# A trunk kernel whose dt columns move beside V's, in products of 320 columns

## The chip, the cores and the metric

The kernel runs on one core of a Trainium2 chip. The metric is device time in microseconds (us), measured over several runs of the same program; beside it stands one profiled execution, whose trace has every instruction with its start, length and engine. The engines are TensorE (PE in the rows; PEld are its weight loads), VectorE (DVE), ScalarE (ACT), GpSimd (POOL) and SyncE (SP, which here issues nearly all DMAs).

## The reference

One layer of a bidirectional hybrid encoder on 512 tokens of width 1024, in float32:

```python
h = rmsnorm(x, pre_mix_norm[l])
proj = h @ w_in[l]
z, xbc, dt_raw, q, k, v, gates = split_cols(proj, IN_SPLITS)
y_ssd = ssd_branch(z, xbc, dt_raw, ...)
y_attn = window_attention(q, k, v, attn_sink[l], rel_bias_table) @ w_attn_out[l]
mixed = (g_ssd * y_ssd + g_attn * y_attn) @ w_o[l]
x = x + rmsnorm(mixed, post_mix_norm[l])
h = rmsnorm(x, pre_mlp_norm[l])
f = jnp.square(jax.nn.relu(h @ w_mlp_in[l])) @ w_mlp_out[l]
x = x + rmsnorm(f, post_mlp_norm[l])
```

Of the columns of `w_in`, two groups matter here. V has 256 (4 heads of 64). `dt_raw` has 64 (32 scan heads in two directions); the scan uses `softplus(dt_raw + dt_bias)`, with `a = -exp(a_log)`. The attention adds a bias that depends on the distance of two tokens alone: a table of 32 x 16, of which the kernel makes a row of 512 distances for each of the 16 heads.

## The kernel before

**Numbers.** Every float32 operand of the large products is split in two parts of a shorter type (fp32r): `hi` is a cast, `lo` is what the cast lost. A product is then three: hi by hi, lo by hi, hi by lo (`mm3`, L393; for V and dt the three are written out). The input is normalised and transposed in four blocks of 128 tokens (`norm_x`, L596): ScalarE and VectorE square one half of the columns each (L603, L604), GpSimd adds and raises to the power -1/2 (L605, L606), VectorE scales by the row factor and by the gain (L609), PE transposes (L391, from `tr`), ScalarE casts the high part (L404) and VectorE subtracts for the low part (L405). The gain row is spread over the partitions by two float32 products of one row (`self.gb`, in `start`).

**Stages.** `start` (L547) loads x and V's weights, issues warm-up products of zeros (`WARM`, and three more), spreads the gain and normalises block 0. Then `build` makes a list of quanta, which `run_quanta` (L512) runs in order: V for each of the four blocks (`v_quantum`), dt (`dt_quantum`), K (2), Q (2), then eight scan groups with attention, gates and more Q between, the output projections and the MLP. Small stages are hung onto a quantum's number with `at(q, fn)`, or `later(d, fn)` counted from the current one: the bias rows (`bias_rows`, L677) at 1, the constant columns (`vectors`, L652) at 4, dt's sums and rows of cumulated decay four and five behind dt.

- `v_quantum(t)` normalises block t + 1, then makes 24 products of 256 columns: the stationary operand is 128 x 128 of the transposed block (high or low), the moving one is V's weights, which `load_v` loads in four pieces of 256 KB (two 128-row tiles each), casts on ScalarE (L575) and subtracts on GpSimd (L576). The 24 go hi by hi, lo by hi, hi by lo, eight each. The result is copied to `V` by ScalarE (L710).
- `dt_quantum` uses the common path for weights (`chunk_raw`, L454, and `chunk_split`, kind "both", L468 and L469): dt's 64 columns, high and low beside each other, make a moving operand of 128 columns against the block's high part, and of 64 columns against its low part, 16 products for each block. `dt_math` adds the halves and the bias (L742, L743) and computes the softplus on VectorE and ScalarE.
- K, Q and the rest take `cm`: eight tiles of weights as the stationary operand, all 512 tokens as the moving one, 24 products. Their raw weights lie in three buffers (`wr`, `RAW`), the split ones in three (`wh`, `wl`, `SPL`), filled ahead by `prefetch`.
- `bias_rows` multiplies the table by a one-hot matrix of distances in one float32 product (33 rows, 16 x 512 out), copies it out on VectorE (L688) and writes it to DRAM (L690), from where each head's bias is loaded (L841).

**Order.** The program order isn't what runs. A `Planner` simulates all instructions with a cost for each, and `chain` fixes its order on every engine. PE takes the first ready product in program order, but stays with one kind (float32 or fp32r) while others have been ready for less than 4 us; the other engines, SP's DMA queue among them, go by deadlines counted back from PE. PSUM has eight banks: three for `pp`, five for `ps`, each used in rotation.

Of the kernel before, what the change touches and what calls it, by code (L numbers as in the profile page):

```python
# [10 lines left out]
F32 = mybir.dt.float32  # L11
# [8 lines left out]
NT = 4  # L20
# [8 lines left out]
LO_DOWN = "p", "p", "p", "vp"  # L29
WARM = 10  # L30

SCAN = dict(load=3, weigh=(-2, -0.5), states=(0, 1), prep=(0, 1.5, 3, 4.5), outs=(2.5, 5.5), rms=9, finish=12,
# [23 lines left out]
class Slots:  # L56
# [5 lines left out]
    def get(self, name, shape=(128, 512), dtype=F32):  # L62
        s = self.free.popleft()
        self.n += 1
        t = self.pool.tile(list(shape), dtype, tag=f"s{s}", name=f"{name}_{self.n}", bufs=1)
        self.tags[t.tensor.name] = f"s{s}", 1
        self.slot[id(t)] = (s, t)
        return t

    def put(self, *tiles):  # L70
        for t in tiles:
            self.free.append(self.slot.pop(id(t))[0])


class Planner:
# [169 lines left out]

    LEAD, TAIL = 1000, 1300

# [7 lines left out]
    def plan(self, wait=0.3):  # L255
# [12 lines left out]
        for _ in self.ins:  # L268
# [17 lines left out]
            t = self.when[n] = max(t, ready[n])  # L286
            c, locks = self.cost[n]
            end = t + c
            if e == "SP":
# [39 lines left out]
class Trunk:  # L329
# [217 lines left out]
    def start(self):  # L547
# [23 lines left out]

        def load_v(k):
            w, hi, lo = (get("wv", (128, 2, 256), d) for d in (F32, F32R, F32R))
            nc.sync.dma_start(w, self.d_w_in[k * 128:(k + 2) * 128, C_V:C_V + 256].rearrange("(k p) n -> p k n", p=128))
            nc.scalar.copy(hi, w)  # L575
            nc.gpsimd.tensor_tensor(lo, w, hi.bitcast(F32), op=ALU.subtract)  # L576
            put(w)
            self.wv.append((hi, lo))

        load_x(0)  # L580
        for k in range(0, 8, 2):
            load_v(k)
        for t in range(1, NT):
            load_x(t)
        self.gb = [self.bank("pp") for _ in range(2)]
        for j in range(2):
            self.mm(self.gb[j], one[:1], g[j][:1], True, True)
        for _ in range(3):
            self.mm(dummy[:, :128], self.zero, self.zero, True, True)
        put(one, *g)  # L590
        self.hb, self.h = self.wide()
        self.norm_x(0)
        self.prefetch(0)
        self.at(1, self.later_constants)
# [100 lines left out]

    def v_quantum(self, t):

        nc = self.nc

        def run(_):  # L700
            if t < 3:
                self.norm_x(t + 1)
            tok = slice(t * 128, (t + 1) * 128)
            ps = self.bank("ps")
            for a, b in ((0, 0), (1, 0), (0, 1)):
                for k in range(8):
                    self.mm(ps[:, :256], self.h[k][a][:, tok], self.wv[k // 2][b][:, k % 2], a + b + k == 0, b == 1 and k == 7)
            if t % 2 == 0:
                self.V.append(self.slots.get("V", (128, 2, 256)))
            nc.scalar.copy(self.V[t // 2][:, t % 2], ps[:, :256])  # L710
            if t == 3:
                for a in self.wv:
                    self.slots.put(*a)

        return Quantum([], run)

    def dt_quantum(self):

        def run(parts):
            ps = self.bank("ps")  # L720
            for t in range(NT):
                tok = slice(t * 128, (t + 1) * 128)
                for k in range(8):
                    hi, lo = self.h[k]
                    self.mm(ps[:, t * 128:(t + 1) * 128], hi[:, tok], parts[0][:, k], k == 0, False, True)
                    self.mm(ps[:, t * 128:t * 128 + 64], lo[:, tok], parts[0][:, k, :64], False, k == 7, True)
            self.dt_math(ps.rearrange("p (t n) -> p t n", t=4))

        return Quantum([(self.d_w_in[:, C_DT:C_DT + 64].rearrange("(k p) n -> p k n", p=128), 8, 64, "both")], run)

    def dt_math(self, ps):
        nc = self.nc
        get, put = self.slots.get, self.slots.put
        bias = self.const("dtb", [128, 2, 64])
        self.bcast_row(bias[:, 0], self.d_dt_bias, 64)
        self.bcast_row(bias[:, 1], self.d_a_log, 64)
        self.tables = [get("tables", (128, 2, 4, 64)) for _ in range(3)]
        self.ncs = self.tables[2][:, 0]
        self.dt, self.cs, self.dec, self.coef = (self.tables[i // 2][:, i % 2] for i in range(4))
        w = [get("dtw", (128, 4, 64)) for _ in range(6)]  # L740
        v, e, r, s2, p, al = w
        nc.vector.tensor_tensor(v, ps[:, :, :64], bias[:, 0].unsqueeze(1).to_broadcast([128, 4, 64]), op=ALU.add)  # L742
        nc.vector.tensor_tensor(v, ps[:, :, 64:], v, op=ALU.add)  # L743

        nc.scalar.activation(e, v, AF.Abs)
# [45 lines left out]

        self.later(4, sums)
        self.later(5, rows)

# [784 lines left out]
    def build(self):  # L1579
# [7 lines left out]
        self.gd = self.dp.tile([1024, 512], F32, name="gd")  # L1587
        self.at(1, self.bias_rows)
        self.at(4, self.vectors)
        self.at(6, self.scan_constants)  # L1590
        kv = self.kv_quanta()
        self.add(*[self.v_quantum(t) for t in range(NT)], self.dt_quantum(), *kv)
        self.add(self.q_quantum(0), self.q_quantum(1))
# [72 lines left out]
```

## Time and profile before

| | us |
|---|---|
| median of 3 runs | 1101.32 |
| lowest, highest | 1098.49, 1101.61 |
| profiled execution | 1102.03 |
| its span, first instruction to last | 1100.0 |
| PE busy in it | 1088.0 |
| ScalarE, VectorE, GpSimd busy | 636.6, 746.4, 774.0 |

The mean granted clock of TensorE over the span was 0.992 of full speed. The busy times overlap, so they don't add up. A row of the timeline gives start, length, engine, line, operation, output tile and input tiles, shape and count; several instructions of one kind in a row are merged. What stands in square brackets at its end is the time for which the engine idled before it, and what ended that.

### The profile page before, as it was taken

The numbers are of one execution on the slowest core, as the hardware profiler recorded it, in microseconds if no ns is written. First come the engines' busy times: TensorE is split into PE (matmuls) and PEld (weight loads), VectorE is DVE, ScalarE is ACT, GpSimd is POOL, SyncE is SP. The second block draws the span as 40 slices with busy tenths as digits, with TensorE's granted clock in tenths as the row PEclk, the third lists the DMA queues.
The fourth block names the chain that finished last, engine by engine and source line by source line (L and its number), as shares of the span: only waits on it lengthen the run. The fifth ranks groups of instructions, "written<-read, shape, count | busy, mean of one in ns | idle before, by whom it ended". The sixth has DMA issues, their size and how long they took to land.

```text
span 1100.0 us, 16840 instructions
## 1 busy us (share of the span) xinstructions
PE 1088.0 (99%) x5664; PEld 914.4 (83%) x5664; DVE 746.4 (68%) x1285; ACT 636.6 (58%) x1364; POOL 774.0 (70%) x965
## 2 busy tenths in 40 slices
PE   9999999999999999999999999999999999999997
PEld 7888888888888888888888878888888888888885
DVE  5467787798797696977788653335653665665787
ACT  5357777777766777676677632323555444444543
POOL 6245657666567898899899775512668978978844
PEclk9899999999999999999999999999999999999999
DMA  7344624535535555556574563535312621621532
GB/s 223 85 114 119 151 75 123 133 85 156 143 97 151 154 161 146 162 149 159 135 196 134 166 208 96 153 100 170 115 40 57 178 77 53 192 75 44 163 101 78
DMA packets 214646, 140.66 MB, mean 128 GB/s; under 512 B 11773, under 2 KB 193509, under 8 KB 214560
## 3 DMA queue, kind: packets, MB, share of 16 engines
q1 hardware_dynamic: 214412, 139.53, 45.5%
q8 instruction: 44, 0.72, 0.3%
q14 instruction: 42, 0.34, 0.1%
q10 hardware_dynamic: 148, 0.07, 0.0%
HBM read 130.85 MB, written 8.72 MB: 127 GB/s over the span
## 4 chain that ended last, share of the span: by engine, by line
PE 96%; DMA 2%; DVE 1%; issue 0%; POOL 0%; POOLq 0%; DVEq 0%; SPq 0%
PE pp L387 67%; PE ps L387 26%; PE ps L391 4%; DMA wd<-in_w_mlp_out 1%; DMA rstd<-rrow 0%; DVE yT L1189 0%; DVE x L1575 0%; DVE acc L1541 0%; DVE junk L609 0%; DVE ag L1568 0%; DVE wd L1459 0%; DVE yl L1236 0%; POOL wl L478 0%; POOLq L1662 0%; DVE wd L1460 0%
## 5 line engine op out<-in xcount | busy, mean ns | idle before, releaser
L387 PE MATMUL pp<-b,wh 128*128 128x512 f32 (+1 forms) x1840 | 565.1, 388 | 0.8 <-DVE h L1331 0.8
L478 POOL TENSOR_TENSOR wl<-wr,wh 128x256 fp32r<-128x256 f32 (+1 forms) x500 | 410.1, 849 | 165.8 <-ACT wh L474 152.0
L387 PEld LDWEIGHTS pp<-b,wh 128*128 128x128 f32 x1840 | 341.3, 188 | 68.8 <-issue 1.0
L387 PE MATMUL pp<-b,wl 128*128 128x512 f32 (+1 forms) x920 | 357.7, 389 | 0.0
L387 PEld LDWEIGHTS pp<-b,wl 128*128 128x128 f32 x920 | 173.4, 189 | 34.9 <-issue 0.3
L474 ACT CAST wh<-wr 128x1024 fp32r<-128x1024 f32 x131 | 136.7, 1044 | 99.2 <-PE pp L387 78.5
L1495 POOL TENSOR_TENSOR wl<-wd,wh 128x256 fp32r<-128x256 f32 x140 | 113.7, 843 | 36.9 <-ACT wh L1491 34.1
L387 PE MATMUL ps<-wh,fh 128*128 128x512 f32 (+1 forms) x196 | 75.5, 385 | 0.5 <-DVE acc L1541 0.5
L1491 ACT CAST wh<-wd 128x512 fp32r<-128x512 f32 x80 | 47.4, 622 | 48.5 <-PE pp L387 26.2
L387 PE MATMUL ps<-wl,fh 128*128 128x512 f32 (+1 forms) x196 | 75.4, 385 | 0.0
L387 PE MATMUL ps<-wh,fl 128*128 128x512 f32 (+1 forms) x196 | 75.4, 385 | 0.0
L1374 DVE SCALAR_TENSOR_TENSOR pp<-pp,r 128x512 f32<-128x512 f32 (+1 forms) x31 | 17.6, 567 | 63.1 <-ACT r L1371 63.1
L1114 ACT ACTIVATE n<-cb,tables 128x128 f32<-128x128 f32 x128 | 49.5, 394 | 16.6 <-DVE cb L1105 14.1
L1495 POOL TENSOR_TENSOR wl<-wt,wh 128x256 fp32r<-128x256 f32 x56 | 45.3, 841 | 9.9 <-PE ps L387 4.9
L1150 POOL TENSOR_TENSOR w<-w,E 128x256 f32<-128x256 f32 x48 | 41.2, 872 | 12.9 <-DVE w L1146 6.5
L946 DVE SCALAR_TENSOR_TENSOR u<-pp,cv,u 128x510 f32<-128x510 f32 (+1 forms) x64 | 47.7, 746 | 3.3 <-ACT u L942 2.1
L1115 ACT ACTIVATE m<-cb,tables 128x128 f32<-128x128 f32 x128 | 49.3, 392 | 0.0
L1044 POOL TENSOR_TENSOR xd<-x,tables 128x256 f32<-128x256 f32 x48 | 35.4, 756 | 16.9 <-ACT x L969 14.1
L866 ACT ACTIVATE P<-P,mx 128x384 f32<-128x384 f32 (+1 forms) x64 | 35.3, 555 | 17.3 <-DVE mx L863 12.2
L1110 ACT ACTIVATE rf<-rf,tables 128x128 f32<-128x128 f32 x128 | 42.5, 396 | 2.4 <-DMA rf<-csT 2.3
L387 PEld LDWEIGHTS ps<-wh,fh 128*128 128x128 f32 x196 | 36.8, 188 | 8.0 <-DVE acc L1541 0.7
L387 PEld LDWEIGHTS ps<-wh,fl 128*128 128x128 f32 x196 | 36.8, 188 | 7.4
(242 smaller groups left out, 2064.0 us busy)
## 6 DMA issues: line engine op xcount, KB each, us to landing
wr<-in_w_in SPq DMA_DIRECT2D x74, 512.0 KB, 4.5
wr<-in_w_mlp_in SPq DMA_DIRECT2D x32, 512.0 KB, 4.2
wd<-in_w_mlp_out SPq DMA_DIRECT2D x64, 256.0 KB, 3.5
rb<-csT SPq DMA_DIRECT2D x32, 256.0 KB, 4.0
rf<-csT SPq DMA_DIRECT2D x32, 256.0 KB, 5.4
wr<-in_w_ssd_out SPq DMA_DIRECT2D x14, 512.0 KB, 4.4
E<-csE SPq DMA_DIRECT2D x96, 64.0 KB, 4.3
x<-in_x SPq DMA_DIRECT2D x16, 256.0 KB, 5.3
```

Source lines behind the costliest of these rows:

```text
L387: self.nc.tensor.matmul(out, lhsT, rhs, start=start, stop=stop, skip_group_check=more)
L391: self.nc.tensor.transpose(out, src, self.ident[:n, :n])
L474: self.nc.scalar.copy(hi[:, :m], raw)
L478: engines[e].tensor_tensor(lo[:, c], raw[:, c], hi[:, c].bitcast(F32), op=ALU.subtract)
L946: nc.vector.scalar_tensor_tensor(u[:, a:e], ps[:, a + d:e + d], self.wtap(t, b), u[:, a:e], op0=ALU.mult, op1=ALU.add)
L1044: nc.gpsimd.tensor_tensor(v4(xd[:, d * 256:(d + 1) * 256]), v4(xs(c)), by_dir(self.coef, c)[:, d].unsqueeze(2).to_broadcast([128, 4, 64]), ...
L1110: nc.scalar.activation(v4(rf)[:, h], v4(rf)[:, h], AF.Identity, bias=ncs[:, 0, h:h + 1])
L1114: nc.scalar.activation(v4(n)[:, h], cb[:, 0], AF.Copy, scale=dt[:, 0, h:h + 1])
L1115: nc.scalar.activation(v4(m)[:, h], cb[:, 1], AF.Copy, scale=dt[:, 1, h:h + 1])
L1150: nc.gpsimd.tensor_tensor(wc, wc, E[:, d], op=ALU.add)
L1491: nc.scalar.copy(hi, w)
L1495: (nc.vector if e == "v" else nc.gpsimd).tensor_tensor(low[:, q], w[:, q], hi[:, q].bitcast(F32), op=ALU.subtract)
```

## The change

- `load_v` now takes up to three 128-row tiles of weights at a time (tiles 0 to 2, 3 to 5, 6 and 7) into one of the raw buffers `wr`, V's 256 columns and dt's 64 beside each other, with a DMA for each group of columns. Each tile of 320 columns is cast on ScalarE by itself; its low part is made on GpSimd or VectorE in turn (`LO_V`).
- `v_quantum` takes a list of blocks. The first quantum has blocks 0 and 1: hi by hi and lo by hi for the one and then for the other, and the products by the weights' low parts last for both. Blocks 2 and 3 follow in a quantum each. Every product has 320 columns; 24 for each block, as before. V's copy takes the first 256 columns, and VectorE adds dt's bias to the other 64.
- `dt_quantum` and its 64 products are gone; `dt_math` follows block 3, and its first addition of halves is gone.
- `start` loads x of block 1 ahead of V's weights in program order, normalises blocks 0 and 1, loads dt's constants, and has four warm-up products behind the gain in place of three. The norm of block 2 is issued inside block 0's products, that of block 3 inside block 2's.
- In the planner, an instruction of PE that starts before 5.3 us costs double.
- `bias_rows` moves from quantum 1 to quantum 3, which is now the first of K's. As there are two quanta fewer ahead of K, dt's sums and rows are hung five and six behind in place of four and five.

```diff
+LO_V = "pvpvpvpv"
...
-    LEAD, TAIL = 1000, 1300
+    COLD, LEAD, TAIL = 5300, 1000, 1300
...
             c, locks = self.cost[n]
+            c *= 2 if e == "PE" and t < self.COLD else 1
...
-        def load_v(k):
-            w, hi, lo = (get("wv", (128, 2, 256), d) for d in (F32, F32R, F32R))
-            nc.sync.dma_start(w, self.d_w_in[k * 128:(k + 2) * 128, C_V:C_V + 256].rearrange("(k p) n -> p k n", p=128))
-            nc.scalar.copy(hi, w)
-            nc.gpsimd.tensor_tensor(lo, w, hi.bitcast(F32), op=ALU.subtract)
-            put(w)
-            self.wv.append((hi, lo))
+        def load_v(k0, k1):
+            w = self.wp.tile([128, 1024], F32, tag="wr", name=self.name("wr"), bufs=RAW)
+            self.tags[w.tensor.name] = "wr", RAW
+            w = w[:, :(k1 - k0) * 320].rearrange("p (k n) -> p k n", n=320)
+            for a, b, c in ((0, 256, C_V), (256, 320, C_DT)):
+                nc.sync.dma_start(w[:, :, a:b], self.d_w_in[k0 * 128:k1 * 128, c:c + b - a].rearrange("(k p) n -> p k n", p=128))
+            for k in range(k0, k1):
+                hi, lo = (get("wv", (128, 320), F32R) for _ in range(2))
+                nc.scalar.copy(hi, w[:, k - k0])
+                (nc.vector if LO_V[k] == "v" else nc.gpsimd).tensor_tensor(lo, w[:, k - k0], hi.bitcast(F32), op=ALU.subtract)
+                self.wv.append((hi, lo))
 
         load_x(0)
-        for k in range(0, 8, 2):
-            load_v(k)
-        for t in range(1, NT):
+        load_x(1)
+        for k in range(0, 8, 3):
+            load_v(k, min(k + 3, 8))
+        for t in range(2, NT):
             load_x(t)
...
-        for _ in range(3):
+        for _ in range(4):
             self.mm(dummy[:, :128], self.zero, self.zero, True, True)
...
         self.norm_x(0)
+        self.dt_bias = self.const("dtb", [128, 2, 64])
+        self.bcast_row(self.dt_bias[:, 0], self.d_dt_bias, 64)
+        self.bcast_row(self.dt_bias[:, 1], self.d_a_log, 64)
+        self.dtv = get("dtw", (128, 4, 64))
+        self.norm_x(1)
...
-    def v_quantum(self, t):
+    def v_quantum(self, some, after):
...
-            if t < 3:
-                self.norm_x(t + 1)
-            tok = slice(t * 128, (t + 1) * 128)
-            ps = self.bank("ps")
-            for a, b in ((0, 0), (1, 0), (0, 1)):
-                for k in range(8):
-                    self.mm(ps[:, :256], self.h[k][a][:, tok], self.wv[k // 2][b][:, k % 2], a + b + k == 0, b == 1 and k == 7)
-            if t % 2 == 0:
-                self.V.append(self.slots.get("V", (128, 2, 256)))
-            nc.scalar.copy(self.V[t // 2][:, t % 2], ps[:, :256])
+            ps = [self.bank("ps" if t else "pp") for t in some]
+            for lowest in (False, True):
+                for t, p in zip(some, ps):
+                    tok = slice(t * 128, (t + 1) * 128)
+                    for a, b in ((0, 1),) if lowest else ((0, 0), (1, 0)):
+                        if (t, a, b) == (some[0], 1, 0):
+                            for u in after:
+                                self.norm_x(u)
+                        for k in range(8):
+                            self.mm(p[:, :320], self.h[k][a][:, tok], self.wv[k][b], a + b + k == 0, b == 1 and k == 7)
+            for t, p in zip(some, ps):
+                if t % 2 == 0:
+                    self.V.append(self.slots.get("V", (128, 2, 256)))
+                nc.scalar.copy(self.V[t // 2][:, t % 2], p[:, :256])
+                nc.vector.tensor_tensor(self.dtv[:, t], p[:, 256:320], self.dt_bias[:, 0], op=ALU.add)
             if t == 3:
                 for a in self.wv:
                     self.slots.put(*a)
+                self.dt_math()
...
-        nc.vector.tensor_tensor(v, ps[:, :, :64], bias[:, 0].unsqueeze(1).to_broadcast([128, 4, 64]), op=ALU.add)
-        nc.vector.tensor_tensor(v, ps[:, :, 64:], v, op=ALU.add)
...
-        self.later(4, sums)
-        self.later(5, rows)
+        self.later(5, sums)
+        self.later(6, rows)
...
-        self.at(1, self.bias_rows)
+        self.at(3, self.bias_rows)
...
-        self.add(*[self.v_quantum(t) for t in range(NT)], self.dt_quantum(), *kv)
+        self.add(self.v_quantum((0, 1), (2,)), self.v_quantum((2,), (3,)), self.v_quantum((3,), ()), *kv)
```

More of the change, by code (lines that the diff above doesn't have):

```diff
@@ L713, in run, with dt_math @@
                     self.slots.put(*a)
+                self.dt_math()
         return Quantum([], run)
[L717 to L731, printed above, removed]
+    def dt_math(self):
         nc = self.nc
         get, put = self.slots.get, self.slots.put
-        bias = self.const("dtb", [128, 2, 64])
-        self.bcast_row(bias[:, 0], self.d_dt_bias, 64)
-        self.bcast_row(bias[:, 1], self.d_a_log, 64)
+        bias = self.dt_bias
         self.tables = [get("tables", (128, 2, 4, 64)) for _ in range(3)]
@@ L739, in dt_math @@
         self.dt, self.cs, self.dec, self.coef = (self.tables[i // 2][:, i % 2] for i in range(4))
-        w = [get("dtw", (128, 4, 64)) for _ in range(6)]
-        v, e, r, s2, p, al = w
-        nc.vector.tensor_tensor(v, ps[:, :, :64], bias[:, 0].unsqueeze(1).to_broadcast([128, 4, 64]), op=ALU.add)
-        nc.vector.tensor_tensor(v, ps[:, :, 64:], v, op=ALU.add)
+        v = self.dtv
+        e, r, s2, p, al = [get("dtw", (128, 4, 64)) for _ in range(5)]
+        w = v, e, r, s2, p, al
         nc.scalar.activation(e, v, AF.Abs)
```

## The prediction

> **What bounds the kernel now.** The page first: its span, the granted clock in 40 slices (tenths of full speed), and the shares of the chain that ended last.
>
> ```profile
> span 1100.0 us, 16840 instructions
> ...
> PEclk9899999999999999999999999999999999999999
> ...
> PE 96%; DMA 2%; DVE 1%; issue 0%; POOL 0%; POOLq 0%; DVEq 0%; SPq 0%
> ```
>
> 96% of the chain that ends last runs through TensorE (PE). So time taken off PE is time off the kernel, unless something late takes its place. One slice of the clock row stands below nine tenths, the second, from 27.5 to 55 us. The profiled execution took 1102.03 us, 2.03 more than its span and 0.7 more than the median of the three runs, 1101.32; the sum below is made against the profiled one. About 0.3% (3.3 us) is what a measurement of this kernel can tell from no change.
>
> Second, PE's timeline of the first 45 us (start, length, engine, line, operands, count, idle before).
>
> ```profile
> 1.03 5.61 PE L387 MATMUL ps<-zero 128*128 128x128 f32 x26 [1.03 <-DVE zero L560]
> 6.57 1.98 PE L387 MATMUL pp<-g,one 1*128 1x512 f32 x4
> 8.71 3.35 PE L391 MATMUL ps<-ident,junk 128*128 128x128 f32 x16 [0.16 <-DVE junk L609]
> 11.72 3.45 PE L387 MATMUL ps<-wv,b 128*128 128x256 f32 x22
> 15.10 1.03 PE L387 MATMUL ps<-hot,tab 33*16 33x512 f32 x2
> 16.06 0.50 PE L387 MATMUL ps<-wv,b 128*128 128x256 f32 x2
> 17.65 1.29 PE L391 MATMUL ps<-ident,junk 128*128 128x128 f32 x8 [1.08 <-DVE junk L609]
> 18.69 3.12 PE L387 MATMUL ps<-wv,b 128*128 128x256 f32 x24
> 21.65 1.21 PE L391 MATMUL ps<-ident,junk 128*128 128x128 f32 x8
> 22.61 5.99 PE L387 MATMUL ps<-wv,b 128*128 128x256 f32 x48
> 28.44 0.63 PE L387 MATMUL pp<-b,wh 128*128 128x512 f32 x2
> ...
> 29.72 10.43 PE L387 MATMUL ps<-wh,b 128*128 128x128 f32 x64
> 39.96 0.77 PE L387 MATMUL pp<-b,wl 128*128 128x512 f32 x1
> ```
>
> Read down: 13 warm-up products (10 and 3; each float32 product is two passes, hence x26), the gain row's broadcast from 6.57, the transposes of blocks 0 and 1 from 8.71, V's 96 products of 256 columns (`ps<-wv,b`) from 11.72, with the bias product (`ps<-hot,tab`) and the transposes of blocks 2 and 3 between them, the first K products at 28.44, and then dt's 64 products (`ps<-wh,b`) from 29.72 until K resumes at 39.96. That is 10.24 us for a thin set of columns.
>
> Third, stretches of one or two times 3.41 us with the granted clock (stretch, length, PE busy and products, clock, DMA share, GB/s).
>
> ```profile
> 6.18:9.59 3.41, 3.22 (x14) 1.00 1.08 372
> 9.59:13.01 3.42, 3.42 (x18) 0.50 1.12 306
> 30.07:33.49 3.42, 3.42 (x33) 1.00 0.51 146
> 33.49:40.31 6.82, 6.82 (x33) 0.50 0.01 2
> 40.31:43.73 3.42, 3.42 (x9) 0.50 0.00 0
> 43.73:47.14 3.41, 3.41 (x16) 1.00 0.45 111
> ```
>
> The clock is at half from 9.59 to 13.01 and again from 33.49 to 43.73. The second time it falls right behind a stretch that holds dt's products alone, stays down while dt's go on, and comes back behind a stretch of K's. In the first case the stretch before it holds the broadcast, products with a single row.
>
> **The change part by part.**
>
> *dt's own products go.* The block of 10.24 us stands on PE with nothing else to run there: the K product behind it starts at its end. Removed: 10.24 us. If K's were otherwise late, this would be worth less, so I look at K's weights below.
>
> *K at half clock.* From 39.96 to 43.73 K's products run for 3.77 us at clock 0.5. By the clock half of that is lost, 1.9 us; by the counts (9 products against 16 in the next stretch) 44%, 1.65. I take 1.8 us. It goes only if dt's products are what pulls the clock down; that is the third rival.
>
> [...]
>
> *V's products grow from 256 to 320 columns.* Their price is read from widths on both sides: 256 columns take (28.44 - 22.61)/48 = 121 ns; 384 columns, in the first attention head, and 512, in a late piece of the chain, are here:
>
> ```profile
> 62.72 0.34 PE L387 MATMUL ps<-KH,Q 128*128 128x384 f32 x1
> 62.90 0.34 PE L387 MATMUL ps<-KL,Q 128*128 128x384 f32 x1
> ...
> 808.90 5.44 PE ps L387 x24
> ```
>
> 384 take 0.18 us from start to start and 512 take 5.44/24 = 227 ns. The three lie on a line; 320 by the line from 256 to 512 is 148 ns, and the bounds are 121 and 180 ns, 0 and 5.7 us for the 96. 96 x 148 = 14.2 us in place of 11.6: **2.6 us more**, all on PE.
>
> *What goes from V's stage.* It now lasts 28.44 - 11.72 = 16.72 us: 11.6 of products, 1.04 + 0.96 of transposes (17.65 to 18.69, 21.65 to 22.61), 0.96 of bias product, 0.65 lost to the half clock up to 13.01, 1.08 idle at 17.65, the rest 0.4 in switching. Why it idles stands in the rows of GpSimd (POOL) and VectorE (DVE):
>
> ```profile
> 10.59 4.22 POOL L576 TENSOR_TENSOR wv<-wv,wv 128x512 fp32r<-128x512 f32 x3 [1.00 <-ACT wv L575]
> 14.77 0.20 POOL L605 TENSOR_TENSOR rst<-ssq 128x1 f32<-128x1 f32 x1
> 15.04 0.54 POOL L606 TENSOR_TENSOR rst<-rst,mhalf 128x1 f32<-128x1 f32 x1
> ```
>
> ```profile
> 16.17 0.68 DVE L688 COPY rows<-ps 16x512 f32<-16x512 f32 x1 [1.31 <-PE ps L387]
> 16.77 1.38 DVE L609 SCALAR_TENSOR_TENSOR junk<-x,rst,pp 128x512 f32<-128x512 f32 x2
> ```
>
> GpSimd makes V's low parts until 14.81; block 2's power waits behind them until 15.58. VectorE then has block 2's scaling (L609) behind the copy of the bias rows (L688), which waits for the bias product: 16.77 instead of some 15.7, and PE waits for it. The change takes all three causes away. Low parts are split between GpSimd and VectorE, four each, and come last, after 32 products (4.7 us); blocks 0 and 1 together give 48 products, 7.1 us, as cover for block 2's norm; the bias product and its copy leave the stage. So the 1.08 us idle and 0.96 us bias go from here. New on the engines: eight casts of 320 columns on ScalarE in place of four of 512, between 0.6 us more (by columns, from the 0.62 us of the row below) and 2.5 us (if each costs as much as a wide one); I take 0.9, nearer the columns. And four subtractions on VectorE, at most 0.7 us each by the wider L688 copy; its four additions of dt's bias take the place of two wider ones. None of these reaches PE while it has V products to run; where they do, it is the late front below.
>
> *The start of V's stage.* The changed planner counts a PE instruction double up to 5.3 us, so by its clock the ten first warm-up products last until the gain row has come, and the broadcast follows them; it can move up by about 1 us, and four warm-up products come behind it. Against that, the first V weights arrive as 480 KB, not 256.
>
> ```profile
> 7.42 0.62 ACT L575 CAST wv<-wv 128x512 fp32r<-128x512 f32 x1 [0.60 <-DMA wv<-in_w_in]
> ```
>
> ```profile
> 13.00:14.00 1.00, 1.00 0.70 116
> ```
>
> Now the first cast waits for its DMA until 7.42. 224 KB more at 372 GB/s, the rate before 9.59, is 0.6 us, so 8.0. The part with dt's columns has rows of 256 bytes; dt's load had them too, and while it was in flight the engines moved 116 GB/s at 0.70 share, 166 at a full one (the second row). In all 256 KB more come ahead of blocks 2 and 3: 0.7 us by the better rate, 1.6 by the worse; I take 1.2. Block 2's norm shifts by that, inside 7.1 us of cover, so PE doesn't see it. dt's two constant rows also load here, 32 KB each, too little to count. The first product: earliest 9.6 (11.72, less 1.0 for the broadcast and 1.1 for block 1's transposes, if these come behind it), latest 12.6 (ScalarE's extra 0.9 all ahead of it). I take 11.2.
>
> *Sum of the stage.* 11.2 + 14.2 + 2.0 transposes + 0.2 switching = 27.6, and 0.9 more if the clock is again at half up to 13.01: 28.5. More dense products now fall into the stretch before 9.59, so I weigh both and take **K's start at 27.9**, 0.5 us earlier than 28.44. Ends: 26.0 (first product at 9.6, full clock) and 30.2 (first at 12.6, half clock to 13.01, 0.8 us of waiting).
>
> [...]
>
> *The bias product behind K.* Its 0.96 us stood partly in a stall; now it interrupts full K work: **1.0 us added** (0 if it fills a wait, 1.3 with two switches). The rows and tables behind it:
>
> ```profile
> 20.67 2.83 POOL L478 TENSOR_TENSOR wl<-wr,wh 128x256 fp32r<-128x256 f32 x4
> ```
>
> ```profile
> 67.55 1.04 PE L387 MATMUL ps<-dtw,cst 128*128 128x128 f32 x6
> ```
>
> The bias rows are first needed by the scores, at 62.72; with some 51 as their new time, a product between 28 and 40 leaves 10 us or more. On SP the write of the rows (L690) now waits later; behind it stand weight loads, three split chunks ahead of PE, 16 us of cover. dt's sums run at 67.55, 27.6 us after dt's products; the changed offsets leave five K and Q products of 5.44 us between, 27 us, as now. K's first weights are split from 20.67 to 23.50, 4.4 us before 27.9, and without dt's chunk GpSimd is free earlier. V's raw weights now share K's three buffers, so K's loads wait for V's casts and subtractions; the 4.4 us cover that. K is not late.
>
> *Further on.* One place has a DMA on the chain:
>
> ```profile
> 750.11 5.96 PE pp L387 x27
> 756.07 5.36 DMA wd<-in_w_mlp_out
> ```
>
> The transfer starts when PE's work ends at 756.07, so it moves with PE, and nothing is given back there.
>
> **Sum:** -10.24 - 1.8 - 0.5 + 1.0 = -11.5 us. 1102.03 - 11.5 = 1090.5; from the median, 1089.8. I forecast 1090.0, between the two.
>
> **The rivals.**
>
> *A clean front.* No half clock before 13 us and the first product at about 10: K starts at 26.4, 1.5 us sooner, 1088.5. For it: the warm-up products behind the broadcast. Against it: ScalarE has to cast V's parts and block 0's transposes in one queue.
>
> *A late front.* V's weights and block 2 come late enough to starve PE: K starts at 30.2, 2.3 us later, 1092.3. For it: rows of 256 bytes at half the rate ahead of x; against it: 7 us of cover.
>
> *The clock falls anyway.* If the half clock from 33.49 to 43.73 is tied to time and not to dt's products, it lies over K's. Of dt's block 6.47 us ran at half clock; at full clock it is 10.24 - 3.2 = 7.0 us, and only that is saved: -7.0 - 0.5 + 1.0 = -6.5, 1094.8. [...] Against it: both falls follow a stretch of thin products, and every other slice of the clock row stands at nine tenths or more.
>
> *Given back.* If one of the DMA steps on the chain, as at 756.07, hangs on an earlier transfer and not on PE, PE comes 11.5 us sooner and waits as much longer: 1101. The PE row right before it speaks against it.
>
> *Slower.* dt's narrow products cost 7.0 us for 32 x 192 columns, 1.14 ns a column, against 0.47 for 256. If 320 columns, no multiple of 128 as V's, K's and the scores' widths are now, are paid at the narrow rate, a product takes 365 ns and the 96 take 35 us, 20.8 more than in the sum: 1110.8. It decides from 300 ns a product on ((11.5 + 3.3)/96 above 148). Against it: the line through 256, 384 and 512.
>
> **How the numbers follow.** Forecast 0.57, clean front 0.18, late front 0.14, clock 0.06, given back 0.03, slower 0.02. The forecast's own range is 1088.9 to 1091.5. The range holds the first three with the run-to-run spread of about 1.5 us at its ends: 1086.5 to 1094.0; 0.11 is left out. Faster by over 0.3%, below 1098.0: the first four, 0.95. Within: 0.03. Slower: 0.02.
>
> **What would show it.** Right: no `ps<-wh,b` block of 64 products; 96 products of 320 columns about 148 ns apart; the first K product near 28 us; the granted clock full from some 13 us on; no idle before block 2's transposes; the bias product among K's. Wrong: a half clock over K (third rival), spacing near 300 ns (last), idle in V's stage over 1 us (late front), or new idle of PE behind 60 us, above all before attention scores, the scan's tables, or at 745 to 760.

## The result, and the profile after

The changed kernel takes 1094.52 us (median of six runs, 1092.37 to 1095.74); the kernel before, on the same chip in the same set, 1102.01 (1098.49 to 1103.70). The ratio is 0.9935 with a 95% interval of 0.9917 to 0.9953: 7.5 us, or 0.65%, faster. Forecast were 1090.0, in a range up to 1094.0; the direction is right, and over a third of the gain is missing.

The page of the changed kernel, its span, clock row and shares of the chain that ended last:

```profile
span 1090.6 us, 16726 instructions
...
PEclk9999999999999999999999999999999999999999
...
PE 29%; DVE 1%; issue 0%; POOLq 0%; POOL 0%; DVEq 0%
```

No slice of the clock row is below nine tenths any more. The row counts the time ahead of the first recorded clock as full: the page of `after_again`, below, shows nines as well, though its products ran at half rate up to 13.5 us. (The chain was followed back over some 30% of the span only, so its shares say less than those of before.) The profiled execution took 1092.37 us, the fastest of the six. It alone can't tell why the median is 2 us higher. PE's timeline in it:

```profile
1.03 4.63 PE L389 MATMUL ps<-zero 128*128 128x128 f32 x20 [1.03 <-DVE zero L562]
5.60 2.28 PE L389 MATMUL pp<-g,one 1*128 1x512 f32 x4
7.80 1.16 PE L389 MATMUL ps<-zero 128*128 128x128 f32 x8
8.80 1.61 PE L393 MATMUL ps<-ident,junk 128*128 128x128 f32 x12
10.90 0.78 PE L389 MATMUL pp<-wv,b 128*128 128x320 f32 x2 [0.48 <-ACT wv L582]
11.51 0.60 PE L393 MATMUL ps<-ident,junk 128*128 128x128 f32 x4
...
13.55 0.54 PE L389 MATMUL pp<-wv,b 128*128 128x320 f32 x2
...
19.03 4.86 PE L389 MATMUL ps<-wv,b 128*128 128x320 f32 x32
23.73 1.04 PE L393 MATMUL ps<-ident,junk 128*128 128x128 f32 x8
25.02 4.03 PE L389 MATMUL ps<-wv,b 128*128 128x320 f32 x24 [0.26 <-ACT b L406]
28.89 0.63 PE L389 MATMUL pp<-b,wh 128*128 128x512 f32 x2
29.45 1.03 PE L389 MATMUL ps<-hot,tab 33*16 33x512 f32 x2
...
52.01 0.28 PE L389 MATMUL ps<-KH,Q 128*128 128x256 f32 x1
...
799.18 0.39 PE L389 MATMUL ps<-wh,fh 128*128 128x512 f32 x1
```

dt's block of 64 is gone and the bias product stands among K's. The 32 products from 19.03 to 23.73 are 147 ns apart. V's first product starts at 10.90, but only four run before 13.55, between groups of transposes; from there PE is dense. In the kernel before, the first score and the first product of the MLP's second half stood here:

```profile
62.49 0.28 PE L387 MATMUL ps<-KH,Q 128*128 128x256 f32 x1
...
808.74 0.39 PE L387 MATMUL ps<-wh,fh 128*128 128x512 f32 x1
```

These marks cut both profiles in four:

| us | before | after | difference |
|---|---|---|---|
| to K's first product | 28.44 | 28.89 | +0.45 |
| K to the first score | 34.05 | 23.12 | -10.93 |
| first score to the MLP's second half | 746.25 | 747.17 | +0.92 |
| from there to the span's end | 291.3 | 291.4 | +0.1 |

So one stretch brings the whole gain, and K starts later, not earlier. In all later profiles the last stretch is 291.4 and the third 746.2 to 747.4; the second is again 23.1 where the bias product stands in K and the clock is full. What differs most from run to run is K's start.

### The profile page after: what moved, and what is told of

Read it like the earlier page. It is cut to its first block, busy times and chain, and to the rows that moved or that the text cites. A ratio compares the mean times of both kernels' runs of the same rounds, so it can differ in the third digit from the quotient of the medians.

```text
span 1090.6 us, 16726 instructions
## 1 busy us (share of the span) xinstructions
PE 1078.6 (99%) x5602; PEld 904.0 (83%) x5602; DVE 743.1 (68%) x1291; ACT 635.8 (58%) x1367; POOL 773.6 (71%) x964
## 5 line engine op out<-in xcount | busy, mean ns | idle before, releaser
L389 PEld LDWEIGHTS ps<-wl,fh 128*128 128x128 f32 x196 | 36.8, 188 | 7.3
```

What stands on the lines that cost most here:

```text
L389: self.nc.tensor.matmul(out, lhsT, rhs, start=start, stop=stop, skip_group_check=more)
```

## The experiments

Each table row is one kernel, with its median, the ratio to the kernel before in the same set (95% interval), and from its profile: when the broadcast of the gain ends on PE, and when K's first product starts. Sets 1 and 4 ran on one chip, 2 and 3 on others; what is compared by its median comes from one set.

| kernel | set | median us | ratio | broadcast ends | K starts |
|---|---|---|---|---|---|
| `narrow_back` | 1 | 1105.39 | 1.0037 [1.0024, 1.0050] | 6.81 | 38.98 |
| `wide_back` | 1 | 1101.36 | 1.0001 [0.9985, 1.0017] | 7.57 | 38.72 |
| `wv_first` | 1 | 1094.00 | 0.9934 [0.9913, 0.9956] | 7.60 | 31.09 |
| `after_again` (changed kernel) | 1 | 1094.38 | 0.9935 [0.9916, 0.9954] | 9.38 | 32.55 |
| `block3_first` | 2 | 1093.58 | 0.9939 [0.9922, 0.9955] | 7.88 | 30.49 |
| `cold_off` | 2 | 1092.39 | 0.9932 [0.9915, 0.9948] | 7.62 | 28.75 |
| `bias_first` | 2 | 1095.08 | 0.9954 [0.9938, 0.9969] | 9.38 | 33.16 |
| `one_by_one` | 2 | 1093.56 | 0.9940 [0.9925, 0.9956] | 9.38 | 30.62 |
| `both_first` | 3 | 1091.51 | 0.9918 [0.9901, 0.9935] | 7.69 | 28.48 |
| `both_cold_off` | 3 | 1092.54 | 0.9925 [0.9907, 0.9942] | 8.16 | 29.55 |
| `both_one` | 3 | 1091.99 | 0.9921 [0.9904, 0.9938] | 7.67 | 28.60 |
| `merge_only` | 3 | 1092.44 | 0.9923 [0.9906, 0.9940] | 8.05 | 30.02 |
| `warm14` | 4 | 1092.46 | 0.9921 [0.9906, 0.9937] | 7.93 | 28.89 |
| `cold_off_ten` | 4 | 1091.75 | 0.9918 [0.9901, 0.9935] | 7.40 | 28.86 |
| `both_warm14` | 4 | 1091.40 | 0.9913 [0.9897, 0.9930] | 8.19 | 29.45 |
| `after_third` (changed kernel) | 4 | 1093.54 | 0.9932 [0.9915, 0.9948] | 9.38 | 31.42 |

### Do dt's narrow products pull the clock down?

Both kernels run 64 more products at the end of V's stage, whose result nobody reads: the one in dt's old shape, the other 256 columns wide.

The one in dt's shape (`narrow_back`), then the wide one (`wide_back`):

```diff
+                extra = self.bank("ps")
+                for u in range(NT):
+                    tok = slice(u * 128, (u + 1) * 128)
+                    for k in range(8):
+                        self.mm(extra[:, u * 128:(u + 1) * 128], self.h[k][0][:, tok], self.wv[k][0][:, :128], k == 0, False, True)
+                        self.mm(extra[:, u * 128:u * 128 + 64], self.h[k][1][:, tok], self.wv[k][0][:, :64], False, k == 7, True)
```

```diff
+                for u in range(NT):
+                    extra = self.bank("ps")
+                    tok = slice(u * 128, (u + 1) * 128)
+                    for k in range(8):
+                        for i in range(2):
+                            self.mm(extra[:, :256], self.h[k][i][:, tok], self.wv[k][0][:, :256], k + i == 0, k == 7 and i == 1)
```

> The changed kernel with 64 extra products between V's and K's, 128 and 64 columns wide in turn, as dt's were; their result is not used. If narrow products pull the clock down: the block lasts about 10 us (full clock for its first 3 to 7 us, half clock behind), K's first products run at half clock until a stretch of 3.41 us is dense again, and the time is 10 to 13 us above the changed kernel's, 1104.5 to 1107.5. If the fall of the clock is tied to a time after the start: the clock stays full, the block lasts 7.2 us, and the time is about 1101.7.

> The changed kernel with 64 extra products in the same place, all 256 columns wide; their result is not used. If width decides: clock full throughout, 64 x 121 ns = 7.7 us more, about 1102.3, more columns than the narrow block in less time. If any 64 products more in this place bring the clock down, or the fall is tied to time: half clock over the block or over K's, 1105 or more.

Windows of `narrow_back`, then of `wide_back` (columns as in the prediction: stretch, length, busy time and instructions of PE, PEld, DVE, ACT, POOL, then clock, DMA share, GB/s):

```profile
31.24:34.65 3.41, 3.41 (x33) 3.41 (x33) 3.12 (x6) 0.34 (x1) 0.00 (x0) 1.00 0.61 163
34.65:48.31 13.66, 13.66 (x42) 10.02 (x42) 5.55 (x13) 0.41 (x2) 0.00 (x0) 0.50 0.18 46
48.31:51.72 3.41, 3.41 (x16) 2.81 (x15) 0.68 (x1) 1.34 (x2) 0.00 (x0) 1.00 0.17 61
```

```profile
32.83:36.24 3.41, 3.41 (x31) 3.41 (x30) 3.24 (x6) 0.00 (x0) 0.00 (x0) 1.00 0.50 148
36.24:39.65 3.41, 3.41 (x27) 3.24 (x26) 3.17 (x8) 0.00 (x0) 0.00 (x0) 1.00 0.00 0
```

Behind a stretch of 3.41 us full of narrow products the clock is at half for 13.66 us; behind one full of wide products, just as busy on PE (3.41 of 3.41 us), it stays at 1.00. Against `after_again` the narrow block costs 11.0 us and the wide one, with more columns, 7.0. The third rival, a clock that falls anyway, is out: the narrow products do it. (The narrow block also writes to one bank and the wide one to four; no run separates that from the width. Nor do 128 columns bring the clock down as such: the warm-up products, in float32, are 128 wide, and the full clock is recorded behind them, from 6.23 us in the changed kernel's profile.)

### Why does K start late?

Two places stand out in the changed kernel. First, ScalarE (ACT) and VectorE (DVE) ahead of block 3's products:

```profile
23.16 1.05 ACT L476 CAST wh<-wr 128x1024 fp32r<-128x1024 f32 x1 [2.18 <-DMA wr<-in_w_in]
24.12 0.36 ACT L726 COPY V<-ps 128x256 f32<-128x256 f32 x1
24.38 1.08 ACT L406 CAST b<-ps 128x512 fp32r<-128x512 f32 x2
```

```profile
25.62 0.17 DVE L653 COPY dcol<-dsk 64x16 f32<-64x16 f32 x1 [0.88 <-DMA dsk<-in_d_skip]
25.71 1.27 DVE L407 TENSOR_TENSOR b<-ps,b 128x512 fp32r<-128x512 f32 x2
```

ScalarE idles 2.18 us for K's second raw weights, with block 3's casts (L406) behind that in its queue; VectorE idles 0.88 us for the constants of d_skip, with block 3's subtractions (L407) behind. Neither is needed yet. Second, V's weights: the first cast waits for its load until 10.39, since SP issues x of blocks 0 to 2 ahead of the six loads.

```profile
10.39 1.18 ACT L582 CAST wv<-wr 128x320 fp32r<-128x320 f32 x3 [0.36 <-DMA wr<-in_w_in]
```

```profile
0.72 2.77 SPq L572 DMA_DIRECT2D x<-in_x  x6
3.78 4.45 SPq L579 DMA_DIRECT2D wr<-in_w_in  x6
8.27 1.18 SPq L572 DMA_DIRECT2D x<-in_x  x2
```

K's raw weights come late, by these rows because V's now lie in the same three buffers: SP issues K's loads right behind VectorE's last reads of them (14.00 + 0.56, and 15.46 + 1.28). In the kernel before, the first two went out at 13.09 and 14.31.

```profile
14.00 0.56 DVE L583 TENSOR_TENSOR wv<-wr,wv 128x320 fp32r<-128x320 f32 x1
...
15.46 1.28 DVE L583 TENSOR_TENSOR wv<-wr,wv 128x320 fp32r<-128x320 f32 x3
```

```profile
14.88 0.40 SPq L456 DMA_DIRECT2D wr<-in_w_in  x1
...
16.83 1.41 SPq L456 DMA_DIRECT2D wr<-in_w_in  x2
```

`wv_first` puts the loads of V's weights ahead of x of block 2 in SP's order:

```diff
+        for n in loads("x_")[4:8]:
+            key[n] = max(key[n], max(key[m] for m in loads("wr_")[:6]) + 1)
```

`block3_first` puts K's second and third cast behind block 3's last cast in ScalarE's order:

```diff
+        for n in writes("wh_")[1:3]:
+            self.turn[n].add(writes("b_")[7])
+            self.next[writes("b_")[7]].append(n)
```

> The changed kernel with V's weights issued on SP ahead of block 2's x, in place of behind it. If the start of V's stage is held by the landing of its weights: the first cast comes about 1.4 us earlier (9.0 in place of 10.4), V's products run without gaps from 12.5 in place of 14, K starts near 27.5, and the time is 1 to 1.5 us below the changed kernel's. If ScalarE's queue holds it, K's start stays at 28.9 and the time is the same.

> The changed kernel again. If the spread between its runs (1092.4 to 1095.7) comes from where a half-clock stretch falls in the first 20 us: a profile that is slower than 1093.5 shows a half-clock stretch of 3.4 us between 9 and 20 us, which the first profile lacks, and its K starts 1 to 1.7 us later. If not: the clock is as in the first profile and the time is lost elsewhere.

> The changed kernel with ScalarE's two casts of block 3 put ahead of the second of K's weight casts, which waits for its load. If this order is what makes PE wait ahead of block 3's products (0.3 to 2.3 us in four profiles): the wait falls below 0.4 us and the time by about 1.2 us, to 1093.2. If the wait is block 3's own norm, it stays and the time is the same.

Both moved the wait instead of removing it. In `wv_first` the first cast comes at 9.15 in place of 10.39, and V's stage is dense from 12.72 and not 13.55, though the clock there is at half from 9.08 to 12.49; but then PE waits for block 2 (first row); in `block3_first` the cast's wait is gone, and VectorE's wait for d_skip is 2.21 us and comes to the surface as 1.42 on PE (second and third).

```profile
16.92 1.29 PE L397 MATMUL ps<-ident,junk 128*128 128x128 f32 x8 [1.31 <-DVE junk L625]
```

```profile
26.93 0.44 DVE L659 COPY dcol<-dsk 64x16 f32<-64x16 f32 x1 [2.21 <-DMA dsk<-in_d_skip]
```

```profile
28.02 2.19 PE L395 MATMUL ps<-wv,b 128*128 128x320 f32 x13 [1.42 <-DVE b L413]
```

`after_again`, the changed kernel once more, showed something else. Its front in PE's timeline:

```profile
1.03 4.64 PE L389 MATMUL ps<-zero 128*128 128x128 f32 x20 [1.03 <-DVE zero L562]
5.60 3.78 PE L389 MATMUL pp<-g,one 1*128 1x512 f32 x4
9.31 2.08 PE L389 MATMUL ps<-zero 128*128 128x128 f32 x8
11.18 2.61 PE L393 MATMUL ps<-ident,junk 128*128 128x128 f32 x12
13.55 0.55 PE L389 MATMUL pp<-wv,b 128*128 128x320 f32 x2
...
21.41 4.86 PE L389 MATMUL ps<-wv,b 128*128 128x320 f32 x32
...
28.02 1.44 PE L389 MATMUL ps<-wv,b 128*128 128x320 f32 x8 [0.88 <-ACT b L406]
30.08 2.63 PE L389 MATMUL ps<-wv,b 128*128 128x320 f32 x16 [0.63 <-DVE b L407]
32.55 0.63 PE L389 MATMUL pp<-b,wh 128*128 128x512 f32 x2
```

The same 10 warm-up products end at 5.60, but the broadcast takes 3.78 us (2.28 in the first profile) and the 8 passes behind it 2.08 (1.16): PE still runs at half rate, and the first full clock is recorded at 13.50, not 6.23. K starts 3.7 us later: V's run of 32 products is 2.4 late (21.41 against 19.03), and the waits ahead of block 3 are 0.88 and 0.63 against 0.26.

### What makes the clock late: the doubled cost, the interleaving, the bias product?

`cold_off` takes the planner's doubled cost away. With it the broadcast goes after 10 warm-up products and four follow; without it 13 go ahead and one follows.

```diff
-    COLD, LEAD, TAIL = 5300, 1000, 1300
+    COLD, LEAD, TAIL = 0, 1000, 1300
```

`bias_first` hangs the bias product back onto V's stage:

```diff
-        self.at(3, self.bias_rows)
+        self.at(1, self.bias_rows)
```

`one_by_one` runs blocks 0 and 1 one behind the other (and hangs the small stages one quantum later, as there is one more):

```diff
-        self.add(self.v_quantum((0, 1), (2,)), self.v_quantum((2,), (3,)), self.v_quantum((3,), ()), *kv)
+        self.add(self.v_quantum((0,), ()), self.v_quantum((1,), (2,)), self.v_quantum((2,), (3,)), self.v_quantum((3,), ()), *kv)
```

> The changed kernel with the planner's doubling of early PE instructions set to zero, so that 13 warm-up products come ahead of the gain's broadcast, as before the change, not 10. If the earlier broadcast helps: up to 1 us slower, 1095.4. If ten warm-up products are too few to bring the clock up in some runs (in one profile it was at half until 13.5 us, and K started 3.7 us later than in another): the clock is full before 8 us in the profile, and the time is the same or up to 1 us lower, 1093.4.

> The changed kernel with the bias product back in the second quantum, among V's products. If its 1 us is paid wherever it stands: the same time within 0.5 us, 1094.4. If it fills a wait of PE in V's stage: 0.5 to 1 us faster, 1093.6. If its copy holds up VectorE ahead of a norm, as before the change: K starts 1 us later and the time is 1 us longer, 1095.4.

> The changed kernel with blocks 0 and 1 in quanta of their own, so that each block's products by the weights' low parts follow its own others. If the interleaving is cover that PE needs: idle of 1 us or more in blocks 0 and 1, K starts 1 to 2 us later, 1095.5 to 1096.5. If the weights' high parts bound the stage's start anyway: the same within 0.5 us.

Without the doubled cost the six runs lie between 1091.98 and 1093.07, the lowest median of the set (the changed kernel itself isn't in it); the clock is full from 4.23 us. `bias_first` and `one_by_one` have the doubled cost, and both profiles show the late clock (13.77 and 13.37). In `bias_first` K to the first score is 22.03, 1.09 less: the bias product's price in K, to be paid in V instead. Its median is the highest of the set, 1.5 us above the other two with the doubled cost; how much of this the place of the bias product makes isn't settled. In `one_by_one` PE idles only 0.24 ahead of block 3: the interleaving isn't needed to cover the norm.

### Both queue waits, and the change cut down

`both_first` holds back K's casts and the d_skip copies behind block 3; `both_cold_off` and `both_one` do so without the doubled cost, the second with the blocks one by one. `merge_only` keeps of the change only dt's columns in V's products, with their loading, dt's constants and block 1's norm in `start`: blocks one by one, bias product in V's stage, no doubled cost, and three warm-up products behind the gain in program order (in its trace all 13 run ahead of it).

```diff
+        hold = [(n, writes("b_")[7]) for n in writes("wh_")[1:3]] + [(n, writes("b_", "DVE")[7]) for n in writes("dcol", "DVE")]
+        for n, m in hold:
+            self.turn[n].add(m)
+            self.next[m].append(n)
```

> The changed kernel with two orders turned round: ScalarE's casts of block 3 ahead of the second of K's weight casts, and VectorE's subtractions of block 3 ahead of the copy of d_skip's columns. With the first alone PE's wait moved to the second queue (1.4 us for VectorE in that profile). If these two waits are what stands ahead of block 3's products: PE waits 0.4 us or less there, and the time is 1 to 1.5 us below the changed kernel's, 1093.2. If another wait takes their place: more than 0.8 us idle ahead of block 3's products, and no gain.

> The same with the planner's early doubling at zero as well. If the two effects are separate and the doubling costs the clock in some runs: narrow spread as in that kernel alone (1092.0 to 1093.1) and 0.3 to 1 us below it, 1091.8. If the early doubling only shifted the same wait: 1092.4 again.

> The same as the last, with blocks 0 and 1 in quanta of their own. If interleaving gives no cover that PE needs: the same time as the last within 0.5 us. If it does: 1 us slower or more.

> dt's columns beside V's alone: no early doubling, three warm-up products behind the gain, no interleaving, the bias product in the second quantum. If the merge brings nearly all of the gain: 1092 to 1095, 7 us or more below the kernel before. If the other parts bring 2 us or more: 1096 or more.

ScalarE in `both_first` shows the order that was wanted, block 3's casts (L412) ahead of K's (L482), with no wait for a load:

```profile
24.22 1.07 ACT L412 CAST b<-ps 128x512 fp32r<-128x512 f32 x2
25.18 2.01 ACT L482 CAST wh<-wr 128x1024 fp32r<-128x1024 f32 x2
```

PE idles 0.24 there. `both_cold_off` shows no further gain over the doubled cost's removal: in its profile the clock is at half from 8.76 to 12.18, and K begins at 29.55. Its expectation named a second outcome, that the doubled cost had only shifted the same wait, and the traces bear it out: in `cold_off`, `cold_off_ten` and `merge_only`, without these edits, PE idles 0.24 ahead of block 3 as well. VectorE in `cold_off` subtracts for block 3 (L407) ahead of the copies (L653) by itself:

```profile
25.11 1.29 DVE L407 TENSOR_TENSOR b<-ps,b 128x512 fp32r<-128x512 f32 x2 [0.43 <-ACT b L406]
26.31 1.24 DVE L653 COPY dcol<-dsk 64x16 f32<-64x16 f32 x2
```

So taking the doubled cost away changes the warm-up and the queues at once, and what the queue waits alone are worth in the median, some 1 us by `warm14` and `both_warm14` below, isn't settled. `merge_only` has the whole gain of the change: 0.9923 [0.9906, 0.9940] against 0.9935, intervals that overlap. Its K starts at 30.02, with the bias product ahead, and its first score at 52.05, as in the changed kernel's own profile (52.01).

### Warm-up products by count

`warm14` keeps the doubled cost and has 14 ahead of the broadcast and four behind; `both_warm14` is `both_first` with the same edit:

```diff
-WARM = 10
+WARM = 14
```

`cold_off_ten` is `cold_off` with ten in all, and all ten go ahead of the broadcast:

```diff
-WARM = 10
+WARM = 6
```

> The changed kernel with 14 warm-up products ahead of the gain's broadcast in place of 10, early doubling as in the change. If the doubling costs because ten products don't always bring the clock up: the profile's clock is full before 8 us, the spread narrows to about 1 us, and the median falls by 1 to 2 us below the changed kernel's of this job. If the doubling costs by the order that it makes elsewhere: no lower than the changed kernel.

> No early doubling, but only ten warm-up products ahead of the broadcast and none behind (13 and one without doubling otherwise). If ten are too few: the spread widens to 2 us or more and the median rises by 1 us or more over the kernel without doubling, 1093.5 to 1095. If the count doesn't matter: about 1092.4 with a spread of 1 us.

> The changed kernel with block 3's casts and subtractions ahead of the two waits, and 14 warm-up products ahead of the broadcast. If the two effects add: 2.5 to 3 us below the changed kernel of this job, 1091 to 1091.8, narrow. If one covers the other: as warm14.

> The changed kernel again, beside the three others on the same chip: 1094.4 with a spread of 2 to 3 us.

`warm14` removes the long runs: 1091.64 to 1092.95, against 1091.83 to 1094.91 in `after_third`, whose profile again shows the late clock (13.28). `both_warm14` has the lowest ratio of the study and is 2.1 us under `after_third` in the same set, but its interval overlaps those of `warm14` and `cold_off_ten`. `cold_off_ten` missed its expectation: with ten products ahead but no doubling its runs stay within 1091.29 and 1092.88.

The profiles together say more than each. The recorded clock changes in steps of 3.41 us (in the kernel before at 6.18, 9.59, 13.01, 33.49 and 43.73, one, one, six and three steps apart). Cut time in such steps, so that one ends where the first full clock is recorded. For the eight profiles below (ten products ahead, broadcast from 5.60), the step in which the broadcast begins holds so much warm-up:

| | step | warm-up in it | full clock from |
|---|---|---|---|
| `wv_first` | 2.25 to 5.67 | 3.35 | 5.67 (to 9.08) |
| `both_first` | 2.45 to 5.86 | 3.15 | 5.86 |
| changed kernel, `block3_first` | 2.82 to 6.23 | 2.78 | 6.23 |
| `after_third` | 3.04 to 6.45 | 2.56 | 13.28 |
| `one_by_one` | 3.13 to 6.54 | 2.47 | 13.37 |
| `after_again` | 3.26 to 6.67 | 2.34 | 13.50 |
| `bias_first` | 3.53 to 6.94 | 2.07 | 13.77 |

The table parts cleanly between 2.56 and 2.78 us, and in every other profile of the study a step ends before the broadcast begins, with 2.8 us of warm-up or more in it. So one reading of the first full clock fits all profiles: the broadcast's products, of a single row, count too little, as steps with 0.85 us of them or more (3.41 less 2.56) are not followed by the full clock and those with 0.63 or less are. At half rate the four passes then last 3.78 us and fill most of the next step as well (to 9.38), and the clock comes two steps late. At half rate a warm-up product lasts 0.46 us (4.64 for ten): by this reading 13 or 14 of them hold a step with 2.8 us of warm-up wherever the steps lie, ten leave about three positions in ten without one (worked out from these rows, an estimate). Where the steps lie differs from run to run: with the same ten products, the steps of the table end between 5.67 and 6.94 us. No run here could set that position, so this stays a reading. It doesn't cover a second effect: of the 13 profiles of the changed kernel and its variants with an early full clock, eight show half clock again for one step behind it (in `wv_first` from 9.08 to 12.49); what decides that wasn't worked out. It also leaves open why `cold_off_ten`, with ten ahead as well, has no long run in six, and why the changed kernel has more than three in ten.

## Why the prediction was off

**Right: what goes from K's stretch.** "dt's own products go" (-10.24), "K at half clock" (-1.8) and "The bias product behind K" (+1.0) make -11.04; K to the first score is 10.93 shorter. The clock is full there (1.00 from 30.1 to 43.7 us), and `narrow_back` beside `wide_back` (0.50 against 1.00) shows that dt's narrow products were the cause; PE was busy for 3.41 of 3.41 us ahead of the fall. The bias product measures 1.09 us by `bias_first`.

**Right: "V's products grow".** 148 ns were forecast, 147 measured; the last rival's narrow rate (300 ns and more) is out. Block 2's idle of 1.08 us went.

**Wrong: "K's start at 27.9".** This is the step that failed. The changed kernel's three profiles have 28.89, 32.55 and 31.42, 1.0 to 4.7 us later. It failed in three terms:

- The broadcast "can move up by about 1 us", counted as pure gain. It did, from 6.57 to 5.60, but the warm-up it displaced was doing work: in two of the changed kernel's three profiles the full clock is recorded from 13.28 and 13.50 us and not from 6.23. In those two K starts 2.5 and 3.7 us later than in the first, with the waits behind it; the sum had "0.9 more" for a clock at half up to 13.01. The runs agree: of the changed kernel's 18 in three sets, 14 are above 1093.1; of the 12 of `cold_off` and `warm14`, none is. But not all 14 need be late: five have a mean granted clock of 0.996, as `wv_first` with its second half-clock step, where the four profiles with the late clock have 0.998.
- V's weights: "so 8.0" for the first cast, measured 10.39. The sum counted the bytes of the weights and took x of block 2 as issued behind them; it goes ahead. The first product's 11.2 was met in the first profile (10.90; 13.55 in `after_again`), but the sum lets all 96 run dense from the first, and PE was dense from 13.55 only. With the other order, in `wv_first`, the first cast came at 9.15: the order explains 1.2 of the 2.4 us, and the rest stays open. It is no better in time, as PE waited for block 2 instead. Rows of 256 bytes weren't as slow as the prediction took them: the 116 GB/s that it read for them, from 13 to 14 us, is from a window in which the transfers run out (365 packets, 189 of them under 512 bytes); the microsecond before it, with 814 of 890 under 512 bytes, moved 272 GB/s, and the changed kernel moves 303 to 356 in each from 8 to 12 us, dt's rows among them.
- "K is not late" and "None of these reaches PE while it has V products to run". K's products were not late; K's *casts* were queued ahead of block 3's, and waited 2.18 us, and 2.81 in `after_again`, for loads that start only when V's raw weights are read. The prediction asked whether K's cover was long enough, not who stands behind the waiting instruction. It costs PE 0.26 us in the first profile (0.24 stay in `both_first` without these waits), 0.88 and 0.63 in `after_again`. V's weights in buffers of their own were not tried.

**Not settled: "nothing is given back there".** The first score to the MLP's second half is 0.9 longer. But over the later profiles this stretch takes 746.2 to 747.4 with no order by kernel (746.23 in `both_first`), and the 746.25 of the kernel before lies in that span, so this isn't shown to be a cost of the change.

**The rivals.** The late front (1092.3) came nearest, but at block 3 and not block 2, by queues and not by rows of 256 bytes. The clock at half from the start to 13.3 us and later was in no case; they had it at half from 9.59 to 13.01 at most. In sum, from the profiled 1102.03: -10.93 in K, +0.45 for K's start, +0.92 and +0.1 further on make -9.4, and the span went from 1100.0 to 1090.6. The median run is some 2 us slower than the profiled one, hence 7.5. The two slower runs that have a profile (1094.91 and 1095.69) show the late clock and the waits behind it; runs near the median have none.

## What to carry to other kernels

When a stage is pulled forward, look at each in-order queue for the instruction that now waits for a load, and at what stands behind it; the cover of the waiting work itself isn't the question. Warm-up products are worth what they do for the clock: keep enough of them ahead of the first thin work, whatever the planner's clock says is free (14 here: no run of `warm14` is above 1092.95, where the changed kernel with its ten reaches 1094.91 in the same set). And fold a thin group of columns into a wider product where one shares its stationary operand: here that step with the loading that it needs (`merge_only`) is worth as much as the whole change (0.9923 against 0.9935).

## What was not expected of the hardware

A stretch of narrow products brought the clock down for 13.66 us in `narrow_back` (0.50 from 34.65 to 48.31); behind wide ones it didn't fall at all (1.00 from 32.83 to 39.65). K's products of 512 columns ran for the last 9 us of these, but not alone:

```profile
38.98 1.20 PE L389 MATMUL pp<-b,wh 128*128 128x512 f32 x2
39.98 0.63 PE L389 MATMUL pp<-b,wl 128*128 128x512 f32 x1
40.54 1.89 PE L389 MATMUL ps<-hot,tab 33*16 33x512 f32 x2
42.35 0.65 PE L393 MATMUL ps<-ident,v 112*128 112x112 f32 x2
42.67 1.20 PE L389 MATMUL pp<-b,wh 128*128 128x512 f32 x2
```

The bias product and two transposes stand among them until 42.67. The first step of 3.41 us with nothing but K's products is the last, 44.90 to 48.31, and the clock is full behind it. In the kernel before it was so too: full from 43.73, behind the step from 40.31 that held K's products alone.

And the times of the kernel before go with its clock: of its 56 runs in the four sets, the 36 with a mean granted clock of 0.990 to 0.993 took 1099.05 to 1103.99 us, the 20 with 0.994 to 0.997 took 1095.34 to 1101.50. The profile of before (0.992) is from the first group, so it shows more half clock than a third of the runs have.
